# One scheduling block with a detailed timing model around the whole body of a two-block transformer kernel

## Chip, cores and metric

The kernel runs on one core of a Trainium2 chip. The metric is the device time of one execution in microseconds (us); less is better. Engines are named as in the profile: PE is TensorE's matmul, PEld its weight load, DVE is VectorE, ACT is ScalarE, POOL is GpSimd, SP is SyncE; SPq and POOLq are the parts of these engines that issue DMAs.

## What is computed

The reference takes x of 1 x 256 x 1024 (f32) through two transformer-like blocks, all in f32:

```
h = rms_norm(x, pre_mix_norm) @ w_in          # 3600 columns: q, k, v | conv input | z | a, b
att = moba_attention(q, k, v, rel_bias)       # 8 heads, causal, T5 position bias
gdn = gated_deltanet(conv+silu, z, a, b)      # 8 heads, chunks of 64, a triangular solve per chunk
x = x + rms_norm(concat(att, gdn) @ w_out, post_mix_norm)
x = x + rms_norm(relu(rms_norm(x) @ w_up)**2 @ w_down, post_mlp_norm)     # 4096 wide
h = rms_norm(x, g_mix_2) @ w_in_2             # 11264 columns: conv branch, retention of 4 heads, gates
x = x + (gated sum of (conv @ w_a_out) and (retention @ w_r_out)) @ w_o
x = x + (silu(rms_norm(x) @ w_gate) * (.. @ w_up)) @ w_down               # 2816 wide
out = rms_norm(x, g_final)
```

In the delta net g = -exp(A_log) * softplus(a + dt_bias), the decays are exponentials of running sums of g within a chunk, and the strictly lower matrix m of each chunk (keys times keys times decay) gives the triangular system that is solved. In the second block dec_f and dec_b go through the same softplus-like function.

## The kernel before

Rows (tokens) are held as two tiles of 128. All weights stay in HBM as f32 and come in 512 KB tiles, one DMA each on the SP queue, into `raw` (3 buffers). ACT copies a tile to the reduced type of the matmuls (`wh`, line 146 called from load_w), DVE forms the remainder `wl = raw - wh` (line 149), 6 buffers each, and every product is three matmuls: wh with xTh, wh with xTl, wl with xTh (line 230). Activations are split in the same way after they were transposed on PE (`xTh` on ACT, `xTl` on DVE).

The order of one engine's instructions is fixed when the kernel is built; each engine then runs its own list in that order and waits at each instruction for what it needs from the others, and a DMA waits in the list of the engine that issues it. The code is written so that generators hand out pieces of the next matrix products ("fill") between the steps of the delta net and of the norms. A few places are held back by hand with `after(...)` (an instruction isn't issued before another one); apart from these the framework's scheduler decides what stands where.

Four stretches matter here; names carry the numbers that the instruction lists print.

1. The start of the delta net. The columns a, b are `abT` (L728, transposed on PE at L731), `xa` adds dt_bias, then log1p_exp_neg_abs (L488 to 507) runs `lpa`, `lpu` on ACT, `lpw`, `lpd`, `lpr` on DVE and the logarithm `lpl` on ACT, which needs another activation table (ACT_TABLE_LOAD). From `g` DVE makes `R_69`, `R_70`, which PE multiplies with constants (`sd_72` to `sd_76`). Meanwhile PE has fill from `w_79`, `w_92` (the weights' numbers) and so on. Normalised keys `kn` are transposed at L802, queries as `qn`, `qd`.
2. The solve. `m` (DVE) is stored to DRAM as `md` (L871, four DMAs on SP), read back as `mb` in another layout (L899), POOL inverts 16 x 16 blocks in a chain of 30 operations on `tb` and copies `ub` (L905), SP stores both (`td` L906, `ud` L907) and loads them as `U`, `T` (L954). Apart from it, queries are copied by ACT from PSUM as `qt_168`, `qdt_170`, `qt_172`, `qdt_174`, and PE multiplies `qt` with the keys `kt` (`sd_181` and following).
3. The end of the mixers. `og_381 = sd_360 * ro_379 * z_271` (two DVE operations) is the gated output of the delta net's second token tile; PE transposes it (`sd_394`), ACT and DVE split it (`mixgh`, `mixgl`) for the products with `w_out`. The first token tile's post-norm is `junk` (squares, ACT, `ss`), `ms` (DVE), `r` (POOL), `pw_418`, `pw_419`, two `x` updates and `xs_420`, `xs_421` (DVE).
4. The start of w_up. rms_norm of the second token tile ends with `ms_441`, `r_442` (POOL), `xs_436`, `xs_437` (DVE), transposes (`sd_443`, `at_444`), `xTh_405` to `xTh_408` and `xTl_409` to `xTl_412`. The products of the second tile are `at_499`. Behind `r_442` POOL issues two small DMAs for `hs_628` (dec_f, dec_b; line 490), on which `lpa_630`, `lpu_631`, `lpl_633` of the second block rest. `relu_496` (ACT) and `hf_497` (DVE) are the first tile's activation.

Of the kernel before, what the change touches and what calls it, by code (L numbers as in the profile page):

```python
# [99 lines left out]
def body(ctx: ExitStack, tc: tile.TileContext, I: dict, cst: bass.AP, out: bass.AP, dbg=None):  # L100
# [11 lines left out]
    psum = ctx.enter_context(tc.tile_pool(name="psum", bufs=1, space=PSUM))  # L112
    dram = ctx.enter_context(tc.tile_pool(name="dram", bufs=1, space=bass.MemoryType.DRAM))

    uid = [0]

    def nm(s):
# [1268 lines left out]
```

## Time and profile before

| | us |
|---|---|
| median of three runs (lowest, highest) | 939.88 (939.13, 941.12) |
| profiled execution, its own time | 941.93 |
| its span in the trace | 940.0 |
| PE busy in the span | 913.8 (97%) |
| PEld, DVE, ACT, POOL busy | 812.4, 559.6, 453.2, 94.4 |
| mean granted clock of TensorE | 0.993 of full |

Busy time is a sum over the span. Matmuls overlap in the pipeline, so their own durations don't add up to the span; the distance from one start to the next tells the pace. What an idle stretch of PE costs is read from its row: the number in square brackets is the idle time ahead of the instruction and the arrow names what it waited for.

### The profile page before, as it was taken

To read this page: it belongs to the slowest core of one execution; us is meant where nothing else is said; L and a number is where in the kernel's file an instruction comes from. 1 tells how busy PE (TensorE), PEld (TensorE's weight loads), DVE (VectorE), ACT (ScalarE), POOL (GpSimd) and SP (SyncE) were. 2 spreads that over 40 slices of the span, in tenths; PEclk is the share of its full clock that TensorE was granted. 3 is DMA by queue.
4 is the path that set the end of the run, shared out by engine and by line. 5 is a ranking of instruction groups with operands and counts; after the bars stand their busy time and mean duration, and the time that the engine had idled before them with its cause. 6 is when DMAs were issued, how large, how long until landed. Compare 5 with 4: busy or idle time off the path is not lost.

```text
span 940.0 us, 15151 instructions
## 1 busy us (share of the span) xinstructions
PE 913.8 (97%) x6096; PEld 812.4 (86%) x6096; DVE 559.6 (60%) x770; ACT 453.2 (48%) x639; POOL 94.4 (10%) x127
## 2 busy tenths in 40 slices
PE   7797999999999999999999999999999999999997
PEld 7697887778999888799988899988888789999886
DVE  3776535486766544768666675645457656555443
ACT  4744464256655443654545554345344545444432
POOL 4187001130000000203200000000000000000000
PEclk9999899999999999999999999999999999999999
DMA  8685542156765666577645466566474567665551
GB/s 216 183 198 148 146 157 90 45 162 174 215 189 190 215 192 197 155 217 210 181 115 176 133 176 184 163 209 191 157 235 142 172 194 201 186 187 185 182 177 45
DMA packets 176870, 161.98 MB, mean 172 GB/s; under 512 B 18916, under 2 KB 144152, under 8 KB 176800
## 3 DMA queue, kind: packets, MB, share of 16 engines
q1 hardware_dynamic: 174912, 155.96, 56.6%
q0 software_dynamic: 1728, 4.78, 1.6%
q8 instruction: 48, 0.79, 0.4%
q10 hardware_dynamic: 160, 0.27, 0.1%
q14 instruction: 22, 0.18, 0.0%
HBM read 158.07 MB, written 2.92 MB: 171 GB/s over the span
## 4 chain that ended last, share of the span: by engine, by line
PE 86%; DMA 4%; DVE 4%; ACT 2%; issue 2%; POOL 1%; SPq 0%; POOLq 0%; ACTq 0%; DVEq 0%
PE mm L230 71%; PE at L230 8%; PE sd L230 7%; DMA raw<-in_w_in_dram 3%; DVE wl L149 1%; DVE acc L152 1%; ACT wh L146 1%; PE sd L802 1%; DMA hs<-in_dec_b_dram 1%; DMA raw<-in_w_up_dram 1%; ACT junk L405 0%; PE sd L1195 0%; POOL r L410 0%; POOL rnk L149 0%; POOL rnq L149 0%
## 5 line engine op out<-in xcount | busy, mean ns | idle before, releaser
L149 DVE TENSOR_TENSOR wl<-raw,wh 128x1024 fp32r<-128x1024 f32 x285 | 348.4, 1227 | 263.5 <-ACT wh L146 262.2
L146 ACT ACTIVATE wh<-raw 128x1024 fp32r<-128x1024 f32 x287 | 302.2, 1056 | 352.3 <-PE mm L230 125.6
L230 PE MATMUL mm<-xTh,wh 128*128 128x256 f32 x960 | 273.1, 286 | 0.2
L230 PE MATMUL mm<-xTl,wh 128*128 128x256 f32 x960 | 272.4, 285 | 0.3 <-DVE xTl L475 0.2
L230 PE MATMUL mm<-xTh,wl 128*128 128x256 f32 x960 | 268.8, 285 | 0.0
L230 PEld LDWEIGHTS mm<-xTl,wh 128*128 128x128 f32 x960 | 185.3, 193 | 1.6 <-DVE xTl L475 0.7
L230 PEld LDWEIGHTS mm<-xTh,wh 128*128 128x128 f32 x960 | 185.2, 193 | 0.8 <-ACT xTh L474 0.6
L230 PEld LDWEIGHTS mm<-xTh,wl 128*128 128x128 f32 x960 | 183.4, 193 | 0.7 <-issue 0.5
L230 PE MATMUL mm<-wh,xTh 128*128 128x512 f32 x264 | 104.0, 394 | 1.2 <-ACT xTh L394 1.2
L230 PE MATMUL mm<-wh,xTl 128*128 128x512 f32 x264 | 103.2, 391 | 1.5 <-DVE xTl L397 1.5
L230 PE MATMUL mm<-wl,xTh 128*128 128x512 f32 x264 | 103.3, 391 | 0.0
L230 PE MATMUL mm<-wh,hidh 128*128 128x512 f32 x162 | 63.3, 391 | 0.1
L230 PE MATMUL mm<-wl,hidh 128*128 128x512 f32 x162 | 63.3, 391 | 0.0
L230 PE MATMUL mm<-wh,hidl 128*128 128x512 f32 x162 | 63.0, 389 | 0.0
L230 PEld LDWEIGHTS mm<-wh,xTl 128*128 128x128 f32 x264 | 49.6, 188 | 12.9 <-DVE xTl L397 2.8
L230 PEld LDWEIGHTS mm<-wh,xTh 128*128 128x128 f32 x264 | 49.6, 188 | 12.3 <-ACT xTh L394 1.9
L230 PEld LDWEIGHTS mm<-wl,xTh 128*128 128x128 f32 x264 | 49.6, 188 | 10.4 <-DVE wl L149 0.5
L410 POOL TENSOR_TENSOR r<-ms,neghalf 128x1 f32<-128x1 f32 x13 | 9.8, 757 | 462.0 <-DVE ms L152 462.0
L230 PEld LDWEIGHTS mm<-wh,hidl 128*128 128x128 f32 x162 | 30.4, 188 | 6.4
L230 PEld LDWEIGHTS mm<-wh,hidh 128*128 128x128 f32 x162 | 30.5, 188 | 6.3 <-issue 0.5
L230 PEld LDWEIGHTS mm<-wl,hidh 128*128 128x128 f32 x162 | 30.5, 188 | 5.6
L405 ACT ACTIVATE junk<-x 128x512 f32<-128x512 f32 x18 | 11.3, 626 | 18.7 <-DVE x L149 12.9
(374 smaller groups left out, 1149.8 us busy)
## 6 DMA issues: line engine op xcount, KB each, us to landing
raw<-in_w_in_dram SPq DMA_DIRECT2D x116, 512.0 KB, 4.5
raw<-in_w_up_dram SPq DMA_DIRECT2D x32, 512.0 KB, 4.5
raw<-in_w_down_dram SPq DMA_DIRECT2D x32, 512.0 KB, 4.3
raw<-in_w_ff_gate_dram SPq DMA_DIRECT2D x22, 512.0 KB, 4.0
raw<-in_w_ff_up_dram SPq DMA_DIRECT2D x22, 512.0 KB, 4.5
raw<-in_w_ff_down_dram SPq DMA_DIRECT2D x22, 512.0 KB, 3.6
raw<-in_w_r_out_dram SPq DMA_DIRECT2D x16, 512.0 KB, 3.8
raw<-in_w_out_dram SPq DMA_DIRECT2D x8, 512.0 KB, 3.5
```

What stands on the lines that cost most here:

```text
L146: nc.scalar.activation(o, i, f, **kw)
L149: (eng or nc.vector).tensor_tensor(o, a, b, op=op)
L152: nc.vector.scalar_tensor_tensor(o, a, s, b, op0=op0, op1=op1)
L230: nc.tensor.matmul(o, a, b, start=start, stop=stop)
L405: last["sq"] = nc.scalar.activation(T2("junk", tag="j"), srcs[i], AF.Square, scale=1.0 / 32, accum_out=ss[:, i:i + 1])
L410: last["pow"] = nc.gpsimd.tensor_tensor(r, ms, neghalf[:, :1], op=ALU.pow)
L802: nc.tensor.transpose(ps[:, a * P:(a + 1) * P], src[:, a * P:(a + 1) * P], ident)
```

## The change

One line is added behind the pools, ahead of the first instruction: the whole body is put into one block of the framework, and that block is scheduled on the framework's detailed timing model of the chip in place of the simpler one that orders it otherwise.

```diff
     dram = ctx.enter_context(tc.tile_pool(name="dram", bufs=1, space=bass.MemoryType.DRAM))
 
+    ctx.enter_context(tc.block(schedule_with_timeline_sim=True))
     uid = [0]
```

The work stays: PE has the same 5686 matmuls, DVE, POOL and SP the same instructions, and ACT has five more ACT_TABLE_LOADs. What moves is the order on each engine, mostly in the first fifth of the matmuls (the mixers of the first block) and in small pieces where one stage passes into the next. Line numbers after it are one higher, and the last number of a name is one higher too.

The SP list around the stores of the solve, before:

```order
L214 DMA raw_232_1246<-in_w_in_dram 128x8x128
L214 DMA raw_254_1382<-in_w_in_dram 128x2x512
L906 DMA td_451<-tb_147_751 128x16x16
L907 DMA ud_452<-ub_148_752 128x16x16
L214 DMA raw_257_1400<-in_w_in_dram 128x2x512
L214 DMA raw_260_1418<-in_w_in_dram 128x2x512
```

and after:

```order
L215 DMA raw_320_1754<-in_w_in_dram 128x2x512
L215 DMA raw_323_1772<-in_w_in_dram 128x2x512
L595 DMA bias_223_1176<-vd_191 128x2x256
L215 DMA raw_326_1790<-in_w_in_dram 128x2x512
L595 DMA bias_251_1379<-vd_191 128x2x256
L907 DMA td_452<-tb_147_752 128x16x16
L908 DMA ud_453<-ub_148_753 128x16x16
L215 DMA raw_330_1814<-in_w_in_dram 128x2x512
L215 DMA raw_354_1910<-in_w_out_dram 128x1024
```

The two stores now stand six weight tiles later, directly ahead of `raw_330`. (The stores of `m` and the load of `mb`, ahead of these rows, moved likewise: from behind `raw_196` and `raw_205` to behind `raw_260`, `raw_267` and `raw_281`.)

ACT's list around the copies of the queries, before:

```order
L146 ACTIVATE wh_233_1248<-raw_232_1246 128x1024
L146 ACTIVATE wh_255_1384<-raw_254_1382 128x1024
L146 ACTIVATE qt_168_855<-sd_169_856 128x512
L146 ACTIVATE qdt_170_862<-sd_171_863 128x512
L548 ACTIVATE y_190_987<-acc_189_986 128x512
L146 ACTIVATE qt_172_869<-sd_173_870 128x512
```

and after:

```order
L147 ACTIVATE wh_327_1792<-raw_326_1790 128x1024
L147 ACT_TABLE_LOAD
L147 ACTIVATE z_270_1493<-mm_252_1381 128x512
L147 ACTIVATE z_271_1495<-mm_253_1382 128x512
L147 ACTIVATE wh_331_1816<-raw_330_1814 128x1024
L147 ACTIVATE qt_168_856<-sd_169_857 128x512
L147 ACTIVATE qdt_170_863<-sd_171_864 128x512
L147 ACTIVATE qt_172_870<-sd_173_871 128x512
```

`qt_168` now stands behind the copy of `raw_330`, the tile whose load stands behind the stores of the solve.

DVE's list at the end of the mixers, before:

```order
L149 TENSOR_TENSOR og_381_2044<-sd_360_1945,ro_379_2040 128x512
L149 TENSOR_TENSOR og_381_2044<-og_381_2044,z_271_1494 128x512
L152 SCALAR_TENSOR_TENSOR mixgl_312_1729<-sd_394_2095,chan_186,mixgh_310_1727 128x2x128
L152 SCALAR_TENSOR_TENSOR mixgl_313_1730<-sd_394_2095,chan_186,mixgh_311_1728 128x2x128
L149 TENSOR_TENSOR pw_418_2189<-mm_350_1905,wb_401_2164 128x512
```

and after:

```order
L150 TENSOR_TENSOR pw_418_2190<-mm_350_1906,wb_401_2165 128x512
L153 SCALAR_TENSOR_TENSOR ms_416_2186<-ss_413_2181 128x1
L150 TENSOR_TENSOR pw_419_2191<-mm_351_1907,wb_402_2166 128x512
L150 TENSOR_TENSOR og_381_2045<-sd_360_1946,ro_379_2041 128x512
L153 SCALAR_TENSOR_TENSOR x_76<-pw_418_2190,r_417_2187,x_76 128x512
L153 SCALAR_TENSOR_TENSOR x_76<-pw_419_2191,r_417_2187,x_76 128x512
L150 TENSOR_TENSOR wl_479_2310<-raw_477_2307,wh_479_2309 128x1024
L150 TENSOR_TENSOR og_381_2045<-og_381_2045,z_271_1495 128x512
```

The second operation of `og_381` stood ahead of the first tile's post-norm and now stands behind it and behind one weight tile's remainder. On PE the transposes `sd_394` stood ahead of the last six rows of `mm_350` and `mm_351`; now they stand behind the last of `mm_351`, with seven rows of the second tile's products between.

ACT's list at the start of w_up, before:

```order
L405 ACTIVATE junk_440_2248,ss_438_2245<-x_75 128x512
L146 ACTIVATE relu_496_2367<-mm_495_2342 128x512
L394 ACTIVATE xTh_405_2172<-sd_443_2256 128x2x128
L394 ACTIVATE xTh_406_2173<-sd_443_2256 128x2x128
L146 ACTIVATE lpa_630_3320<-hs_628_3316 128x8
L394 ACTIVATE xTh_407_2174<-at_444_2265 128x2x128
```

and after:

```order
L406 ACTIVATE junk_440_2249,ss_438_2246<-x_76 128x512
L147 ACTIVATE lpa_630_3321<-hs_628_3317 128x8
L147 ACTIVATE lpu_631_3322<-lpa_630_3321 128x8
L147 ACTIVATE relu_496_2368<-mm_495_2343 128x512
L502 ACT_TABLE_LOAD
L502 ACTIVATE lpl_633_3324<-lpw_632_3323 128x8
L395 ACTIVATE xTh_405_2173<-sd_443_2257 128x2x128
L395 ACTIVATE xTh_406_2174<-sd_443_2257 128x2x128
```

The chain on `hs_628` now stands ahead of all four copies `xTh` of the second tile. POOL's list is the same there: `r_442`, then the two DMAs of `hs_628`.

## Rows read from the trace of the kernel before

**Rows 1.** The page: busy time of each engine (share of the span).

```profile
PE 913.8 (97%) x6096; PEld 812.4 (86%) x6096; DVE 559.6 (60%) x770; ACT 453.2 (48%) x639; POOL 94.4 (10%) x127
```

**Rows 2.** What PE waited for, over the span: total, times, longest (us).

```profile
PE at L230 <- ACT aqk L146: 2.7, 1, 2.7
PE sd L802 <- DVE kn L149: 2.5, 2, 1.8
PE sd L230 <- DVE R L149: 2.3, 1, 2.3
PE sd L802 <- DVE qn L149: 1.8, 1, 1.8
...
PE sd L731 <- DVE abT L728: 1.5, 1, 1.5
...
PE sd L802 <- ACT qt L146: 1.1, 1, 1.1
```

**Rows 3.** PE by stretch: span, busy time (instructions), granted clock, DMA share, GB/s.

```profile
45.00:50.00 5.00, 4.40 (x21) 0.66 0.38 104
75.00:80.00 5.00, 3.88 (x41) 1.00 0.05 18
...
95.00:100.00 5.00, 5.00 (x25) 0.50 1.01 240
100.00:105.00 5.00, 5.00 (x79) 0.88 0.62 184
```

**Rows 4.** PE in order of time: start, us, instruction [idle before <- releaser].

```profile
57.03 0.28 PE L230 MATMUL mm<-xTl,wh 128*128 128x256 f32 x1
57.15 0.28 PE L230 MATMUL mm<-xTh,wl 128*128 128x256 f32 x1
```

**Rows 5.** ACT in order of time, start of the delta net.

```profile
25.23 1.28 ACT L501 ACT_TABLE_LOAD   x1
26.52 0.22 ACT L501 ACTIVATE lpl<-lpw 128x16 f32<-128x16 f32 x1
```

**Rows 6.** DVE in order of time, same stretch and the last m.

```profile
30.10 1.28 DVE L149 TENSOR_TENSOR R<-g,cs 128x512 f32<-128x512 f32 x2
...
54.16 0.42 DVE L149 TENSOR_TENSOR m<-sd,eb 128x256 f32<-128x256 f32 x1
```

**Rows 7.** POOL in order of time: first step of the solve chain.

```profile
68.03 0.23 POOL L149 TENSOR_TENSOR tmpb<-mb,tb 128x15 f32<-128x15 f32 x1 [1.65 <-DMA mb<-md]
```

**Rows 8.** SP queue in order of time, and ACT behind its load.

```profile
83.34 0.37 SPq L906 DMA_DIRECT2D td<-tb  x1
...
89.51 1.06 ACT L146 ACTIVATE wh<-raw 128x1024 fp32r<-128x1024 f32 x1 [6.57 <-DMA raw<-in_w_in_dram]
```

**Rows 9.** DVE in order of time, end of the mixers.

```profile
190.87 0.68 DVE L149 TENSOR_TENSOR pw<-mm,wb 128x512 f32<-128x512 f32 x1
191.63 1.42 DVE L152 SCALAR_TENSOR_TENSOR x<-pw,r,x 128x512 f32<-128x512 f32 x2
...
194.16 1.22 DVE L149 TENSOR_TENSOR wl<-raw,wh 128x1024 fp32r<-128x1024 f32 x1
```

**Rows 10.** ACT in order of time, start of w_up; then POOL and PE there.

```profile
212.86 0.21 ACT L146 ACTIVATE lpa<-hs 128x8 f32<-128x8 f32 x1 [3.42 <-DMA hs<-in_dec_b_dram]
...
205.79 1.40 POOL L410 TENSOR_TENSOR r<-ms,neghalf 128x1 f32<-128x1 f32 x1 [4.07 <-DVE ms L152]
...
208.82 0.60 PE L433 MATMUL at<-ident,xs 128*128 128x128 f32 x4
...
209.73 0.40 PE L230 MATMUL mm<-wh,xTl 128*128 128x512 f32 x1
209.96 0.39 PE L230 MATMUL at<-wh,xTh 128*128 128x512 f32 x1
```

**Rows 11.** DMA issues: KB each, median us from issue to landing.

```profile
hs<-in_A_log_dram POOLq DMA_DIRECT2D x1, 4.0 KB, 2.8
...
hs<-in_dec_b_dram POOLq DMA_DIRECT2D x1, 2.0 KB, 5.1
```

## Prediction

> **What bounds the kernel now.** The page first: PE is busy 97% of the span, no other engine over 60% but the weight load that runs under PE [rows 1]. All that another order can win is therefore PE's idle time and its slow stretches, and all that it can lose is new idle time of PE; the work itself is the same. So the next view is what PE waited for over the whole span [rows 2]: the list is short, and nearly all of it stands between 18 and 95 us, in the start of the delta net. Six entries matter: aqk 2.7, kn 2.5, R 2.3, qn 1.8, abT 1.5, qt 1.1 us, together 11.9. The third view, PE by stretch, shows what follows two of them: after the kn waits the granted clock is 0.66 in 45 to 50 us, after the aqk wait it is 0.50 in 95 to 100 and 0.88 in 100 to 105 [rows 3]. Lost there, as (1 - clock) x busy time: 0.34 x 4.4 = 1.5 us, and 0.50 x 5 + 0.12 x 5 = 3.1 us. **At most 11.9 + 1.5 + 3.1 = 16.5 us** are to be had, 1.8% of the span; everything after 230 us runs with PE full.
>
> **The change part by part.** What it removes: the transposes of abT, the kn, qn and aqk steps stand 25 to 185 rows of PE's list later, with weight products put ahead of them. A product row of 256 columns takes 0.12 us (two neighbouring starts, [rows 4]), so the kn transposes, 120 rows later, have some 14 us of cover for a 2.5 us wait. I count all 16.5 us as gained and then add the waits that the new order makes. The cover is not free: these products were the fill of the later steps.
>
> *R and w_92, +4.1.* In the new ACT list two table loads and y stand ahead of lpl, and DVE has a weight remainder and the convolution's sums ahead of xa. In the trace a load takes 1.28 us and lpl starts at its end [rows 5]; R started at 30.10 [rows 6]. Behind the first weight remainder that is no earlier than now, I add the operations of the new lists one by one (one more remainder at 1.22, [rows 9], one more table load 1.28, y and the sums about 1) and get R 3.4 us later. PE comes there 1.5 us earlier (no abT wait) and has 26 more rows, 3.1 us, to do first. Wait before 2.3 + 3.4 + 1.5 - 3.1 = 4.1 us. Bounds: 2.3 (nothing later) and 5.5 (the fill, w_92 itself, is stuck behind lpl on the same ACT list).
> The Trainium skill, page "ScalarE: Activation LUTs", section "What ACT_TABLE_LOAD costs", gives a switch 1283 ns and a drain of some 1380 ns on top. The trace agrees with the load alone: the next ACTIVATE starts 1.29 us after the load's start [rows 5]; by the page's sum each of the two switches on this path and the one at w_up would make the wait 1.4 us longer, 2.8 to 4.1 us in all.
>
> *The queries, +5.0 and +3.1.* This is the stall I trust most in kind and least in size. qt_168, qdt_170, qt_172 now stand on ACT behind the copy of raw_330, whose load stands on SP behind the stores td and ud, which wait for POOL's chain, which waits for m. From the last m (54.16, [rows 6]) to the chain's first step (68.03, [rows 7]) it was 13.9 us, from there to the store td (83.34, [rows 8]) 15.3, from there to the end of the first weight copy behind it (89.51 + 1.06) 7.2, and one copy of qt about 0.5: 36.9 us from m to qt. m comes later, since PE's key products stand about 147 rows later; adding the rows at their pace gives 18 us, less 3.7 us of waits that are gone by then, plus about 2 for its place in DVE's list: m at 70.5, qt at 107.5. PE reaches sd_181 184 rows later than before; with its rows added up and the same waits taken off it is there at about 102. Wait about 5.4; since both ends move with the same early waits I take 5.0, with bounds 1 and 9. The same queue is passed by U and T, loaded four tiles later, but their users stand another hundred rows on: nothing. Behind a wait of that length I count a slow stretch like the one after aqk, 3.1 us; bounds 0 and 3.1.
>
> *Small waits of the solve's end, +1.0* (0 to 2): one accumulator of the state products comes free behind a DVE remainder of 1.22 us that stood elsewhere.
>
> *og_381, +4.7.* Its second operation now waits behind pw_419, og's own first operation, the two x updates and one remainder. By [rows 9], pw_419 ends at 191.55, then 0.68 (as for pw, the same shape) + 1.42 + 1.22 + 0.68, less overlaps of about 0.1, = 195.5. PE finished mm_351 at about 190.0 and then has seven rows, at 0.23 us each (209.73 to 209.96, [rows 10]) 1.6 us: it stands from 191.6 to 195.5, 3.9 us, and another 0.8 until ACT and DVE split the transposed tile. Bounds 2.5 (the remainder's copy is early and overlaps) and 5.
>
> *The first xTh of w_up, +1.0* (0 to 2): two weight copies of about 1.06 us stand ahead of a copy xTh or junk; the other engine's work hides one of them.
>
> *lpa at w_up, +6.3 and +3.1.* All copies xTh of the second tile stand behind lpa, lpu, relu, a table load and lpl, and lpa waits for hs, whose DMAs POOL issues right behind r. The trace has both ends: r starts at 205.79, lpa can start at 212.86, 7.1 us later, while now the copies go ahead of it [rows 10]. Then 0.2 + 0.2 + 0.6 + 1.28 + 0.2 + 0.4 for lpu to the first xTh, less overlaps: 215.5 on this clock. PE has done its transposes by 209.2 (208.82 and four of 0.09) and has no row in between, where it had a few: a wait of 6.3 us where the trace has none (the row 209.96 shows no idle time). The landing behind dec_b was 5.1 us, that behind the like A_log 2.8 [rows 11]; with 2.8 the wait is 4.0, the lower bound. A slow stretch after it: 3.1 (0 to 3.1). DVE's xTl stand behind lpw, lpd, lpr, which are done in that time.
>
> Further on the list changes by small swaps where w_down ends and where w_o ends; PE's waits there are none of the six largest, and I leave it at 0, with 2 either way.
>
> Sum: -16.5 + 4.1 + 8.1 + 1.0 + 4.7 + 1.0 + 9.4 = **+11.8 us**. The profiled execution took 941.93, so 953.7; it is 2.05 us above the median of the runs, 939.88, and by the median that is 951.7, **952 us**.
>
> **The rivals.**
> *Half speed behind every wait.* The waits for R and og_381 are longer than the 2.65 us one that was followed by half clock, so they too could be: 2 x 3.1 = 6.2 more, 958. Against it: the 2.3 us wait for R and the 1.8 + 1.1 us at qn were followed by none (1.00 in 75 to 80 us, [rows 3]), and before og_381 PE is full. The Trainium skill, page "TensorE: Matmul & The Clock Gate", section "HAM oscillation — how this bites in real kernels", says that waits for data ahead of each block let the clock fall each time, so that every block starts at half rate; by it this case would be the rule, and the trace has it after two waits and not after two others.
> *Not slower: the DMA round trips are shorter than they were.* The landings around 80 to 95 us were slow because the loads of U and T and three weight tiles ran together (DMA share 1.01 even at 95 to 100, [rows 3]). Now they stand apart. If m to qt takes under 31.5 us in place of 36.9, the query wait of 5.0 and its 3.1 vanish, and if hs lands in 2.8 as A_log did, 2.3 of the lpa wait go, and its slow stretch of 3.1 may: 13.5 less, 938. It decides at the md and mb trip: with that alone the time is 944, still slower. For it: the spread of landings; against it: 15.3 us of the trip are POOL's own steps, and SP's new tiles stand ahead of md and mb.
> *The fill is spent.* The solve's tail (U, Q, T products, each waiting for ACT or DVE) has less weight work between its steps than before. If three such steps wait 1.5 to 2 us each, about 5 more, 957. Against it: the new list still has several rows of w_327 and w_331 between them.
> That the change does nothing is no case: the lists themselves differ.
>
> **How the numbers follow.** The sum as made 0.60, half speed everywhere 0.12, shorter round trips 0.20, spent fill 0.08. A difference under 0.2% (1.9 us) is what a measurement of this kernel can't tell from none. The third case lies about 938 with a spread of 4: 0.13 faster, 0.05 within, 0.02 slower. In the first, if all four waits with wide bounds come out near their lower ends at once (1, 4.0, 2.5, 2.3, no slow stretch), the sum is -16.5 + 2.3 + 1 + 2.5 + 4.0 = -6.7; I give that 0.05, of which 0.04 is faster. So faster 0.17, within 0.06, slower 0.77. The range that leaves out 2 in 10 goes from 937 to 962: below by the third case, above by half speed with the upper bounds of the query and R waits.
>
> **What would show it.** Right: no PE wait for abT, kn, qn or aqk; PE waiting 3 to 5 us for a copy wh or R near 30 us; one wait of 3 to 8 us near 105 us released by ACT qt, with ACT idle before it on the DMA of raw; one for og near 195 to 205, released by DVE; one of 4 to 7 us at the start of w_up released by ACT xTh, with ACT waiting for hs; a granted clock under 0.7 behind two of them. Wrong: if qt is released before PE comes, or if PE shows a long list of waits of 1 to 2 us in the solve's tail; and if PE's idle time after 230 us grows by more than 2 us, the small swaps that I left at 0 were the point.

## The result: 1.2% slower

Four executions each on one chip: 951.35 us (949.48 to 952.45) against 940.07 (939.13 to 941.12), a ratio of 1.0115 (95% interval 1.0101 to 1.0129). The forecast was 952. The profiled execution of the changed kernel happens to be its fastest, 949.48 us with a span of 947.7 and a mean granted clock of 0.996; the three others had 0.987 to 0.990. That matters below: some of what this trace shows is at its mildest. Two executions among the runs below, one of 13 of the kernel before and one of 10 of mixers_mended_2, took some 1113 us at a mean granted clock of 0.75; they count in no ratio.

The page's first part after the change, the answer to [rows 1]:

```profile
span 947.7 us, 15171 instructions
PE 913.7 (96%) x6096; PEld 811.0 (86%) x6096; DVE 563.0 (59%) x770; ACT 459.0 (48%) x644; POOL 91.0 (10%) x127
```

PE is busy as long as before to 0.1 us; the span of this pair is 7.7 us longer by the time that PE stands. What PE waited for (total, times, longest, us), the answer to [rows 2]:

```profile
PE sd L803 <- DVE og L150: 3.7, 1, 3.7
PE mm L231 <- DVE xTl L398: 2.9, 2, 1.5
PE mm L231 <- DVE acc L153: 2.7, 1, 2.7
PE mm L231 <- ACT xTh L395: 2.7, 3, 1.8
...
PE mm L231 <- ACT wh L147: 2.5, 1, 2.5
PE sd L803 <- ACT qt L147: 1.8, 1, 1.8
PE at L231 <- ACT xTh L395: 1.7, 1, 1.7
PE mm L231 <- DVE mgl L153: 0.8, 1, 0.8
...
PE mm L231 <- ACT mgh L395: 0.6, 1, 0.6
PE mm L231 <- ACT mixgh L395: 0.6, 1, 0.6
PE sd L803 <- DVE kn L150: 0.5, 1, 0.5
```

abT, R, qn and aqk (ahead of the logits) are gone from the list and kn is down from 2.5 to 0.5; in their place stands a longer list. (The first wait of the kernel, for the constant `ident`, is 2.5 us in this execution and 1.6 in every other profile.) The slow stretches moved too, from 45 to 50 and 95 to 105 us [rows 3] to behind the wait for og; up to 190 us the clock is full in this execution (PE by stretch: span, busy time, granted clock, DMA share, GB/s):

```profile
45.00:50.00 5.00, 4.98 (x42) 1.00 0.57 159
95.00:100.00 5.00, 5.00 (x24) 1.00 0.43 152
100.00:105.00 5.00, 5.00 (x34) 1.00 0.54 59
190.00:195.00 5.00, 1.75 (x6) 0.69 0.31 100
195.00:200.00 5.00, 5.00 (x16) 0.63 0.37 113
```

### The profile page after: what moved, and what is told of

Read it like the earlier page. It is cut to its first block, busy times and chain, and to the rows that moved or that the text cites. A ratio compares the mean times of both kernels' runs of the same rounds, so it can differ in the third digit from the quotient of the medians.

```text
span 947.7 us, 15171 instructions
## 1 busy us (share of the span) xinstructions
PE 913.7 (96%) x6096; PEld 811.0 (86%) x6096; DVE 563.0 (59%) x770; ACT 459.0 (48%) x644; POOL 91.0 (10%) x127
## 4 chain that ended last, share of the span: by engine, by line
PE 80%; ACT 2%; DVE 2%; issue 1%; DMA 1%; POOL 0%; POOLq 0%; DVEq 0%; ACTq 0%
PE mm L231 66%; PE at L231 7%; PE sd L231 5%; ACT wh L147 1%; DVE wl L150 1%; ACT junk L406 0%; PE sd L803 0%; DMA raw<-in_w_up_dram 0%; PE sd L1196 0%; DMA hs<-in_dec_b_dram 0%; ACT lg L147 0%; DVE xTl L398 0%; DVE x L153 0%; DVE mr L153 0%; DVE pw L150 0%
```

## The experiments

A local change of the code makes the scheduler order everything anew, so the experiments set the order itself. At the end of the body each instruction of PE, DVE, ACT and SP gets an edge to the one that shall stand ahead of it on its engine (an edge of issue order, no wait); POOL is left to the scheduler, and its list differs from before in 3 places or fewer. The table ORDER holds the places in a list of before or after, or a mixture:

```diff
+    for e, rows in ORDER.items():
+        have = mine[e]                      # this engine's instructions as traced
+        for p, q in zip(rows, rows[1:]):
+            tc.add_manual_dep(have[q], have[p].name, mybir.DependencyInfo(
+                mybir.DependencyClass.NoSync, mybir.DependencyReason.DATA), reason="order")
```

All of these kernels are the kernel before with this addition, without the block, so line numbers are those of before. (A block without the detailed model was not run; that its five lists are those of before, instruction by instruction, rests on the lists alone.)

### Is it the order? And which stretch of it?

The two sets of lists have places where they hold the same instructions so far, and can be cut there: at the end of the solve (PE 1110, DVE 194, ACT 139 instructions, SP from its 58th on alike) and after the start of w_up (1326, 252, 182). I call the three pieces the mixers, the handover and the rest.

> The kernel before, without the block and on the simpler model, but PE, DVE, ACT and SP are each told to issue in exactly the order that the changed kernel has (POOL is left to the scheduler). Theory 'order': the change acts through these four orders alone, so 949 to 953 us and the same waits (og near 3.7, acc near 2.7, wh near 2.5). Rival 'block': the block itself (its entry, buffer choices, POOL) carries part, then 941 to 947.

Measured: 953.04 us (952.62 to 954.24), ratio 1.0143 (1.0125 to 1.0161). The lists carry the whole effect; the rival "block" falls. It is even 1.7 us above the changed kernel, with intervals that just overlap (1.0101 to 1.0129 against 1.0125 to 1.0161); whether POOL's few places or the choice of buffers make that is left open. One expected wait did not come: in place of the one for acc, 2.75 us at 77 us in the changed kernel, stands one of 1.52 for aqk at 75 us, so in this one place the run is not the changed kernel over again. Its profiled execution, 953.2 us, lies near the median, and here the wait for qt is long (what PE waited for, then PE by stretch):

```profile
PE sd L802 <- ACT qt L146: 4.8, 1, 4.8
PE sd L802 <- DVE og L149: 3.7, 1, 3.7
PE mm L230 <- ACT xTh L394: 3.2, 3, 2.2
PE mm L230 <- DVE xTl L397: 2.9, 2, 1.5
PE mm L230 <- ACT wh L146: 2.5, 1, 2.5
```

```profile
30.00:35.00 5.00, 2.56 (x5) 0.78 0.05 15
35.00:40.00 5.00, 5.00 (x23) 0.88 0.80 214
110.00:115.00 5.00, 3.78 (x41) 0.66 0.63 215
195.00:200.00 5.00, 3.80 (x12) 0.67 0.69 195
```

Each of the three long waits (wh near 32 us, qt near 111, og near 196) has a slow stretch behind it. The queue behind the wait for qt, on SP, ACT and PE in order of time:

```profile
102.30 0.37 SPq L906 DMA_DIRECT2D td<-tb  x1
...
109.62 1.06 ACT L146 ACTIVATE wh<-raw 128x1024 fp32r<-128x1024 f32 x1 [6.89 <-DMA raw<-in_w_in_dram]
110.58 0.58 ACT L146 ACTIVATE qt<-sd 128x512 f32<-128x512 f32 x1
...
111.22 1.05 PE L802 MATMUL sd<-ident,qd 128*128 128x128 f32 x4 [4.83 <-ACT qt L146]
```

> The orders of the changed kernel from the start to where the solve ends (PE's first 1110 matmuls, DVE's first 194, ACT's first 139, all of SP's moved DMAs), the orders of before from there on. Theory 'handover': by the two traces PE is about 3 us ahead of before when it reaches the transposes of og_381, and loses 9 behind that; so the first stretch alone gives 935 to 938. Rival 'mixers': the new waits for acc, wh and qt are what costs, so 943 or more.

Measured: 940.17 us, ratio 0.9996 (0.9978 to 1.0014). Neither figure: the mixers alone are a wash. PE's waits up to 190 us that are over 0.3 us add up to 0.42 + 2.50 + 0.47 + 0.73 + 1.52 + 0.46 + 0.47 + 0.49 = 7.1 us behind its start, against 11.9 of before [rows 2]: 4.8 of the gain that I had in mind. In the clock this execution loses as much as before:

```profile
30.00:35.00 5.00, 2.73 (x6) 0.84 0.03 8
35.00:40.00 5.00, 5.00 (x24) 0.82 0.83 224
60.00:65.00 5.00, 4.15 (x35) 0.91 0.65 167
65.00:70.00 5.00, 5.00 (x44) 0.50 0.55 145
70.00:75.00 5.00, 5.00 (x48) 0.91 0.61 156
```

As (1 - clock) x busy time that is 0.4 + 0.9 + 0.4 + 2.5 + 0.5 = 4.7 us, as much as the 4.6 that before lost in other places [rows 3]. The slow stretches were not removed, they came behind other waits. So the clock does not explain where the 4.8 us went. The two profiled executions are 3.3 us apart (938.67 against 941.93), and the gain does show between them; but they lie 1.5 us below and 1.9 above medians that are the same, and what the mixers take differs from one execution to the next: in the seven profiles whose lists are those of the changed kernel up to there, PE starts the first transpose of an og between 171.6 us (og_early) and 177.1 (og_and_split_early). How much a typical execution gains in waits and loses in clock stays open.

> The orders of the changed kernel up to the first products of w_up (PE's first 1326 matmuls), the orders of before from there on. Theory 'handover': what stands further on costs about 2 us of the change, so 948 to 951. Rival 'far stages': the small swaps at the ends of w_down and w_o cost most of it, so under 944.

Measured: 948.24 us, ratio 1.0091 (1.0073 to 1.0109), in the theory's range, though what stands further on makes 4.8 us against all_after_orders, not its 2. With the mixers at 940.17, the handover from the mixers to w_up costs 8.1 us. The traces agree: from the first transpose of an og to the first of an hf (the activation of w_up) PE takes 43.7 us here and 35.8 in after_mixers, which has two rows more to do there.

> The opposite piece: the orders of before up to the first products of w_up, those of the changed kernel from there on. Theory 'handover': 941 to 943, with the waits for mgh, mgl and xTl of 0.6 to 1.5 us that the changed kernel shows near 392, 727 and 753 us. Rival 'far stages': 946 or more. If both halves together don't add up to the whole, the pieces act on each other.

Measured: 944.21 us, ratio 1.0045 (1.0028 to 1.0062), 4.2 us over the 939.99 of before beside it and between the two figures. So the three pieces are 0.2 + 8.1 + 4.2 = 12.5, the whole was 13.1: they add up. The far stages, which the prediction left at 0, cost as much as the forecast's term for R (4.1). One of their waits, on PE and on DVE just ahead of it (in the changed kernel, order of time):

```profile
750.30 2.35 DVE L150 TENSOR_TENSOR wl<-raw,wh 128x1024 fp32r<-128x1024 f32 x2
752.57 0.74 DVE L398 TENSOR_TENSOR xTl<-sd,xTh 128x256 fp32r<-128x256 f32 x2
```

```profile
753.04 0.50 PE L231 MATMUL mm<-wh,xTl 128*128 128x512 f32 x1 [1.40 <-DVE xTl L398]
```

Two weight remainders stand ahead of xTl, which PE waits for. The same pair makes 1.50 us at 391.7, and ACT's copies and DVE's remainders ahead of mgh and mgl make 0.63 and 0.77 near 727; each was 0.4 or nothing before. In the profile of this run the four are up by 3.7 us together, and the clock behind the first is 0.83 in 380 to 390 us, 1.4 us more as (1 - clock) x busy time.

### The single suspects, one at a time

These start from all of the changed kernel's orders (953.0 us) and move a few rows.

> The orders of the changed kernel, but DVE's two operations of og_381 stand ahead of pw_418, as they did before. Theory 'each wait costs itself and the slow clock behind it': the wait for og (3.7 us), the one for mixgh (0.6) and the slow stretch at 195 to 200 us (0.33 x 3.8 = 1.3) go: 953.0 - 5.6 = 947 to 948. Rival 'next in line': pw_418 and x come later by the same 1.4 us and the first products of w_up wait instead, so 950 or more.

```diff
 TENSOR_SCALAR ms_380_2041<-oss_378_2038 128x8
+TENSOR_TENSOR og_381_2044<-sd_360_1945,ro_379_2040 128x512
+TENSOR_TENSOR og_381_2044<-og_381_2044,z_271_1494 128x512
 TENSOR_TENSOR pw_418_2189<-mm_350_1905,wb_401_2164 128x512
```

(with the two rows taken out further down). Measured: 951.2 us (949.97 to 953.4), 1.8 us better by the medians and not clear of noise (ratios 1.0089 to 1.0135 against 1.0125 to 1.0161). The wait did leave og, and went to the next step of the same chain (PE in order of time):

```profile
187.97 0.63 PE L802 MATMUL sd<-ident,og 128*128 128x128 f32 x4 [0.53 <-DVE og L149]
191.81 0.50 PE L230 MATMUL mm<-wh,mixgh 128*128 128x512 f32 x1 [3.21 <-ACT mixgh L394]
```

```profile
190.67 0.63 ACT L405 ACTIVATE junk<-x 128x512 f32<-128x512 f32 x1
191.21 0.19 ACT L405 ACTIVATION_READ_ACCUMULATOR junk<-x 128x1 f32 x1
191.30 0.82 ACT L394 ACTIVATE mixgh<-sd,chan 128x256 fp32r<-128x256 f32 x2
```

On ACT the split of og stands behind the squares of x, thus behind the same post-norm. The rival was right that the next in line waits, though it named another place.

> The orders of the changed kernel with og_381 early on DVE as in the run before, and now its split too: ACT's two mixgh behind junk_415 and DVE's two mixgl behind the x updates. Theory 'the whole chain og, transposes, split stood behind the post-norm': the wait of 3.7 us goes and does not come back at mixgh (3.2) and mixgl (1.2), so 947 to 948.5 against 951.2 with og alone and 953.0 with neither. Rival 'next in line': the later copies or xs make the first products of w_up wait as much, 950 or more.

```diff
 ACTIVATE junk_415_2183,ss_413_2180<-mm_351_1906 128x512
+ACTIVATE mixgh_310_1727<-sd_394_2095,chan_186 128x2x128
+ACTIVATE mixgh_311_1728<-sd_394_2095,chan_186 128x2x128
 ACTIVATE wh_478_2308<-raw_477_2306 128x1024
```

(and the two mixgl on DVE behind the x updates). Measured: 953.85 us (950.76 to 958.16): nothing is left of the gain. og, mixgh and mixgl wait 0.5 to 0.7 us each, and now the first products of w_up wait for xTh, by 5.5 us in the profiled execution, since ACT's list has weight copies ahead of it that wait for their loads:

```profile
203.83 1.06 ACT L146 ACTIVATE wh<-raw 128x1024 fp32r<-128x1024 f32 x1 [0.99 <-DMA raw<-in_w_up_dram]
...
206.94 1.06 ACT L146 ACTIVATE wh<-raw 128x1024 fp32r<-128x1024 f32 x1 [0.90 <-DMA raw<-in_w_up_dram]
207.91 0.64 ACT L394 ACTIVATE xTh<-sd 128x256 fp32r<-128x256 f32 x2
```

The totals mix the handover with what the mixers took in each execution, so it is read by itself, from the first transpose of an og to the first of an hf (starts in us, one trace each):

| run | og | hf | between |
|---|---|---|---|
| after_mixers | 172.92 | 208.74 | 35.8 |
| all_after_orders | 176.03 | 219.67 | 43.6 |
| og_early | 171.57 | 216.48 | 44.9 |
| og_and_split_early | 177.07 | 221.71 | 44.6 |
| lpa_late (the next run) | 174.88 | 218.44 | 43.6 |

None of the mends made it shorter. What og_early is ahead of all_after_orders it had at og already (4.5 us), with a wait of 2.1 us for qt in place of 4.8. So the 8.1 us of the handover are not the place of one row. The lists of before take all of it away as a whole (after_mixers against after_to_w_up), mending it link by link did not.

> The orders of the changed kernel, but lpa, lpu and lpl (ACT) and their DVE operations stand behind the split of the second token tile and of hidh. Theory 'by the trace': only the wait of 1.65 us for xTh goes, so 951 to 952. Rival, the prediction's own figure (6.3 and 3.1 of slow clock): 944 to 945.

```diff
-ACTIVATE lpa_630_3320<-hs_628_3316 128x8
-ACTIVATE lpu_631_3321<-lpa_630_3320 128x8
 ACTIVATE relu_496_2367<-mm_495_2342 128x512
-ACTIVATE lpl_633_3323<-lpw_632_3322 128x8
 ACTIVATE xTh_405_2172<-sd_443_2256 128x2x128
```

(set in again behind hidh_446; on DVE lpw to lg behind hidl_460). Measured: 952.01 us (949.71 to 953.01), against 953.0: within 1 us and not clear of noise (ratios 1.0091 to 1.0137 against 1.0125 to 1.0161), and far from the 9.4 of the prediction. The wait of 1.65 us is gone from the profile; the handover took as long all the same (the table above), with a clock of 0.66 in 205 to 210 us, 1.2 us, where all_after_orders had it full.

> The orders of the changed kernel, but the weight copy wh_331 stands behind qdt_174 on ACT, so that the copies of the queries no longer wait for raw_330. Theory 'queue head': the wait of 4.8 us for qt and the slow stretch at 110 to 115 (0.34 x 3.8 = 1.3) go, 953.0 - 6 = 947. Rival 'the solve sets it': the same chain holds U, so PE waits for aqk or U products a little later, 951 or more.

```diff
-ACTIVATE wh_331_1815<-raw_330_1813 128x1024
 ACTIVATE qt_168_855<-sd_169_856 128x512
 ACTIVATE qdt_170_862<-sd_171_863 128x512
 ACTIVATE qt_172_869<-sd_173_870 128x512
 ACTIVATE pt0_276_1534<-at_278_1536 128x512
 ACTIVATE pt1_277_1535<-at_279_1537 128x256
 ACTIVATE qdt_174_876<-sd_175_877 128x512
+ACTIVATE wh_331_1815<-raw_330_1813 128x1024
```

Measured: 947.07 us (946.71 to 952.0), 6 us better than 953.0, as expected, and clear of it (ratios 1.0047 to 1.0108 against 1.0125 to 1.0161). In the profile PE no longer waits for qt and comes to the first transpose of an og at 168.97 us, in place of 176.03. One row on ACT, a weight copy that waits for a load that waits for a store that waits for POOL, was worth nearly half of the whole loss of 13.1. The "solve sets it" rival falls.

### A list that beats both

> The orders of the changed kernel up to the solve's end, those of before behind it (940.2 us as it stood), with two more pieces mended: ACT's first 36 and DVE's first 52 instructions as before, so that lpl, R and wh_92 come early, and wh_331 behind qdt_174. Theory 'early fill pays once its own waits are gone': without the 2.5 us wait for wh_92 and the slow stretch at 30 to 40 us (0.4 + 0.9) it takes 935 to 937. Rival 'one wait for another': PE then waits for R, aqk or acc as much, 939 to 941.

ACT's list against that of after_mixers, at the start (weight copies and accumulators behind the steps that lead to R) and at the queries (cut; the first rows are named by their last numbers alone):

```diff
-ACTIVATE acc_316<-mm_191,chan 128x256 x2
-ACTIVATE wh_422<-raw_420 128x1024
 ACTIVATE beta_265<-ab_258 128x16
 ACTIVATE lpa_269<-xa_263 128x16
 ACTIVATE lpu_270<-lpa_269 128x16
+ACTIVATE wh_422<-raw_420 128x1024
...
-ACTIVATE wh_331_1815<-raw_330_1813 128x1024
 ACTIVATE qt_168_855<-sd_169_856 128x512
...
 ACTIVATE qdt_174_876<-sd_175_877 128x512
+ACTIVATE wh_331_1815<-raw_330_1813 128x1024
```

Measured: **932.77 us** (932.13 to 935.31), ratio to before 0.9919 (0.9891 to 0.9946): 7.4 us faster than before, 18.6 faster than the changed kernel. PE waits up to 190 us now add up to 0.30 + 1.26 + 0.47 + 1.52 + 0.46 + 0.47 + 0.49 = 5.0 us, and of the first 240 us the clock was below 0.97 only in 170 to 180. So the new idea in the changed kernel's order, weight products ahead of the delta net's early steps, does pay, by more than I had expected.

> The mended mixers (932.8 us) without the move of wh_331: only ACT's first 36 and DVE's first 52 instructions as before. Theory 'queue head': PE, 4 us earlier at the queries, now waits there for qt by 4 to 6 us, with some slow clock, so 937 to 940, and the gain of the two mends is not a sum of two. Rival 'the start alone': the wait for wh_92 was all, and 932 to 934 stay.

The first half of that diff without the second, wh_331 back ahead of qt_168. Measured: 937.54 us (936.06 to 941.71), ratio 0.9988 (0.9969 to 1.0006). The theory's range; the queue head again: PE came earlier and waited for qt, with the clock at 0.66 behind it:

```profile
105.78 0.44 PE L802 MATMUL sd<-ident,qd 128*128 128x128 f32 x2 [2.72 <-ACT qt L146]
```

By the medians the two mends are worth 2.6 us (the start, 940.17 to 937.54) and 4.8 (wh_331, to 932.77). The second is clear of noise (0.9891 to 0.9946 against 0.9969 to 1.0006), the first is not (0.9978 to 1.0014 before it); in the one trace of each, PE starts the first transpose of an og at 172.92, 170.65 and 166.29 us.

> The mended mixers with two more ACT moves: y_68 ahead of the weight copy wh_156, aqk_199 ahead of wh_258. Theory 'queue head': the waits of 1.26 us for y and 1.52 us for aqk shrink to 0 and 0.3, so 930 to 931. Rival 'noise of the clock': a slow stretch somewhere outweighs 2.5 us, 932 to 935.

```diff
-ACTIVATE wh_156_800<-raw_155_798 128x1024
 ACTIVATE y_68_389<-acc_67_388 128x512
+ACTIVATE wh_156_800<-raw_155_798 128x1024
```

(and wh_258 behind aqk_199 likewise). Measured: 935.08 us, the median of nine executions (932.47 to 939.56), ratio 0.9955 (0.9936 to 0.9973): no better, and nearer to the rival. The wait for y is gone, that for aqk down to 0.7; PE comes 1.2 us earlier to the next step, whose time DVE sets, and stands there instead (0.47 before this move):

```profile
51.41 0.36 PE L230 MATMUL mm<-xTh,wh 128*128 128x256 f32 x1 [1.72 <-DVE ms L383]
```

and in this execution the clock is at half speed from 65 to 70 us, which it was not in the run without the two moves.

## Why the prediction came out right, and where its steps did not

**The total was right, and partly by luck.** By pieces it read -3.3 for the mixers (the 16.5 gained, less 4.1, 8.1 and 1.0), 15.1 for the handover (4.7, 1.0, 9.4) and 0 for the rest; measured 0.2, 8.1 and 4.2. Two misses of 3.5 and 4.2 us on one side met one of 7 on the other. In the changed kernel's own profiled execution, its fastest, the mixers came out as forecast: counted through PE's 6096 matmul records, the 1451st starts 3.3 us earlier than in the profile of before, the 1701st (behind the start of w_up) 5.7 later and the last 7.4 later, so -3.3, +9.0 and +1.7. The piece that moves most between executions is the mixers.

**Gained waits: right; gained clock: wrong as a rule.** abT, R, qn and aqk vanish and kn shrinks, as summed. The 4.6 us of slow clock vanished in two of the eight profiles with the changed start (the changed kernel's own and og_early); in the others it came back elsewhere, 4.7 in after_mixers. The step at fault is "I count all 16.5 us as gained": slow stretches belong to the waits of an order, and every new order with waits has its own. The rival "half speed behind every wait" was nearer here than the chance of 0.12 that I gave it. The wait of 2.5 us for wh_92 is followed by a clock below 0.95 in six of the eight profiles in which it stands; that of 3.7 for og in all five; the wait for qt where it is 2.7 us or longer in all five, and not where it is 1.8 or 2.1. The Trainium skill, page "TensorE: Matmul & The Clock Gate", section "HAM oscillation — how this bites in real kernels", tells of a kernel in which PE waits for data ahead of every block and every block then starts at half rate. The traces agree for the longer waits here; behind the two short ones for qt the clock stayed full.

**R and w_92: within the bounds, by the other cause.** 4.1 with bounds 2.3 and 5.5; the wait is 2.49 us and is for wh_92, the case named for the upper bound, and it has a slow stretch as a rule. On ACT the copy starts right behind lpl (31.35 behind 31.23 us in all_after_orders). R came 2.5 us later than before (32.57 against 30.10), not 3.4, and PE did not wait for it. What the prediction did not have are the waits at 75 us: 2.75 for acc in the changed kernel, 1.52 for aqk in the runs (in both a weight product of PE stands behind a DVE or ACT operation further down its list; that it waits for an accumulator to be emptied is my reading).

**The queries: right in kind, both ends late.** 5.0 us with 3.1 of slow clock: 1.76 in the changed kernel's profiled execution, 4.8 in the run with its orders, 2.1, 3.7, 4.6 and 5.5 in others, and 0.2 in after_mixers, where PE came later by its own slow stretch at 65 to 70 us; 6 us came back in qt_early. The sum put the last m at 70.5 us, PE at 102 and the end of qt at 107.5 (36.9 us behind m). In the changed kernel and in all_after_orders m came at 75.8 and 75.7, PE at 107.7 and 106.4, and qt was done at 109.5 and 111.2, 33.6 and 35.5 us behind m. PE was 4 to 6 us late and qt 2 to 4, so the wait was close to its figure because both ends moved, as I had allowed for.

**og_381: the size right, the consequence wrong.** 3.74 + 0.56 against 3.9 + 0.8, row for row (DVE, then PE, in the changed kernel):

```profile
191.85 0.69 DVE L150 TENSOR_TENSOR og<-og,z 128x512 f32<-128x512 f32 x1
...
192.68 1.09 PE L803 MATMUL sd<-ident,og 128*128 128x128 f32 x4 [3.74 <-DVE og L150]
```

But I treated it as a term that could be taken away, and two runs showed that the chain behind it (mixgh, xTh) stands in the same queues.

**lpa: wrong by 7.7 us.** Two steps failed. First the landing: it took 2.7 us, not the 5.1 of before, the lower bound that I had named from A_log [rows 11]. It is no scatter: it took 2.7 to 3.0 in all seven profiles with the changed lists there and 4.4 to 5.5 in the six others. In before three weight loads stand on SP in the 2.7 us ahead of it and the DMA share of the 3 us behind the issue is 0.88; in the changed kernel the last weight load was issued 4.3 us ahead and the share is 0.37.

```profile
hs<-in_dec_b_dram POOLq DMA_DIRECT2D x1, 2.0 KB, 2.7
```

Second, I kept PE's distance from r as it was, 3.4 us to the end of its transposes; in the changed kernel r starts at 209.52, and PE is through its transposes 4.8 us later, at about 214.3. Counted from the last row of w_out (197.58 us before, 201.70 now), r comes 0.4 us earlier than before and the end of the transposes 1.0 later; in between PE stands 1.80 us for the first xTh, where it stood 0.24 for xTh and 0.90 for xTl. A smaller part is r's own operation, 0.56 us in place of 1.40. ACT's side came as worked out (POOL, PE, ACT, PE):

```profile
209.52 0.56 POOL L411 TENSOR_TENSOR r<-ms,neghalf 128x1 f32<-128x1 f32 x1 [2.85 <-DVE ms L153]
...
213.92 0.60 PE L434 MATMUL at<-ident,xs 128*128 128x128 f32 x4
...
213.42 0.21 ACT L147 ACTIVATE lpa<-hs 128x8 f32<-128x8 f32 x1 [4.25 <-DMA hs<-in_dec_b_dram]
...
214.37 1.28 ACT L502 ACT_TABLE_LOAD   x1
215.66 0.21 ACT L502 ACTIVATE lpl<-lpw 128x8 f32<-128x8 f32 x1
215.78 0.64 ACT L395 ACTIVATE xTh<-sd 128x256 fp32r<-128x256 f32 x2
...
216.20 0.50 PE L231 MATMUL at<-wh,xTh 128*128 128x512 f32 x1 [1.68 <-ACT xTh L395]
```

lpa to the first xTh took 2.4 us, against 2.6 added up; ACT idled 4.25 us, PE only 1.68, with no slow stretch. Here too lpl starts 1.29 us after the table load began, with no drain on top, against the sum on the Trainium skill's page "ScalarE: Activation LUTs", section "What ACT_TABLE_LOAD costs", that the prediction weighed.

**The far stages: wrong.** "PE's waits there are none of the six largest, and I leave it at 0": the waits of before say nothing on what a swap makes. Four of them grew by 0.6 to 1.2 us, and with the clock behind them they cost 4.2. This is the prediction's own last sign of being wrong, PE's idle time after 230 us up by more than 2 us: the waits over 0.2 us there add up to 2.0 us before and 5.2 in the changed kernel.

**The signs.** Of the others, the waits that should be gone are gone or, for kn, small. The wait near 30 us is 2.5, under the 3 to 5 named; that for qt is 1.8 in the changed kernel's profile, under the 3 to 8, and 4.8 in all_after_orders; og came at 193 us, released by DVE as named; the 4 to 7 us for xTh did not come. One wait of the changed kernel's profile, og's, has a clock under 0.7 behind it; two were named, and all_after_orders shows two (qt and og). Why the detailed model put these rows where it did, and what times it took for them, no run here shows.

## What to carry to other kernels

Where one engine is busy 97% of the span, another order has little to win and much to lose, and a wait is best read as a queue: go from the waiting instruction to what stands ahead of it on each engine's list, down to a DMA or a slow engine; one weight copy in the wrong place was worth 6 us. A wait that is removed where several lists run in step can turn up at the next step, as it did in og_early, og_and_split_early and mixers_mended_2; there a whole stretch of the lists could be exchanged where single links could not. A gain of 2 us is read from the stretch that was changed, since the total carries what all other waits did in that execution. And a scheduler's order need not be taken or left as a whole: cut where both lists hold the same instructions, keep the better piece; here the parts added up to within 0.6 us.

## What was not expected of the hardware

The same lists give different waits in different executions: the wait for qt stood at 1.8 us in one execution and at 4.8 and 5.5 in others with the same lists up to there, and those had a granted clock of 0.66 and 0.50 in the 5 us behind it where the first had 1.00. Part of the difference is in the trip of m through DRAM: from the last m to POOL's first step it took 11.2 and 11.5 us where the wait was 2.1 and 1.8, and 12.7 to 13.4 where it was 3.7 to 5.5. A 0.73 us wait for kn was followed by half speed from 65 to 70 us in after_mixers, and so were waits of 0.86 and 0.57 in mixers_mended_2, while the same wait of 0.57 in all_after_orders was not; what decides that these runs don't show.
